# The first sum of weight blocks follows its first low part at once on VectorE, and the third query group is copied one tile sooner

## The chip, the cores and the metric

The kernel runs on one core of a Trainium2 chip. The metric is device time in microseconds; lower is better. The time before is the median of three runs.

Engine names as in the profile: PE is TensorE's matmul side, PEld its weight loads, DVE is VectorE, ACT is ScalarE, POOL is GpSimd, and SP issues DMAs (its queue is SPq).

## What is computed

A trunk of two residual layers over 256 tokens of width 2048, in float32. Layer 0 mixes the tokens by stick-breaking attention (16 heads), layer 1 by a selected sparse softmax attention with 16 query heads in four groups, each group with one key and value head. After each mixer comes an MLP with a squared ReLU. Cut to what matters:

```python
for i in range(DEPTH):                       # DEPTH = 2
    h = rms_norm(x, norm_mix[i])
    x = x + (stick_breaking_mixer(h, w_in_a, w_out_a) if i % 2 == 0 else
             dsa_mixer(h, w_in_b, w_out_b, q_norm_b, k_norm_b, rel_bias))
    h = rms_norm(x, norm_mlp[i])
    x = x + jnp.square(jax.nn.relu(h @ w_up[i])) @ w_down[i]     # 2048 -> 8192 -> 2048
return x
```

## The kernel before

**High and low parts.** Every weight tile (128 x 1024 float32, 512 KB) comes by DMA as a raw tile. ACT copies it to a rounded format as its high part (`wh`, line 121, called by `high`), DVE subtracts that from the raw tile and leaves the low part (`wl`, line 1200, in `low`). PE multiplies by the high part first, then by the low part. Activations are split alike, so a product is three matmuls where a plain one would be one.

**Items.** The whole program is a list of items, each one weight tile with its matmuls. A main loop walks the list. At item i it traces the low part of item i + 3, then loads, then the high part of item i + 4, then the matmuls of item i, and then the steps posted to item i. The traced order is not the order of issue: a planner with a model of the times orders each engine's instructions afterwards, and takes, when an engine comes free in the model, the ready instruction that was traced first. `keep_in_program_order` (here also `pin`) fixes one instruction behind the one traced just before it on the same engine, in issue order alone; it adds no wait. From item 16 on low parts are not fixed. Each engine carries out its own stream in order.

**Groups by halves.** An MLP's hidden width is worked in eight tiles of 1024. The first is done plainly. Each of the seven others (function `seven`, once per f in 1 to 7, in both layers: 14 groups) forms its up-projection from halves of the width and of the tokens, with seven products in place of eight, from sums of weight blocks and sums of activation blocks. Such a group goes over the width in four steps. A step's first half has four items, called here A, B, C and D:

- A uses the block `b11` as loaded (raw tile in `wraw`), into `pair(0)` of an `acc` tile;
- B uses `b22` as loaded (`sraw`), with summed activations `xS`, into the `aux` tile "v";
- C uses b11 + b12, made in place in b11's tile by `two` (line 503), with `xS`, into the `aux` tile "z";
- D uses b12 + b22, made in b12's tile by `other` (line 507), into `pair(1)`. After D's low part comes `three` (line 511), which adds b11 to b22's tile.

Before the change `two` is the source function of item C: it is called when C's high part is made, in `high`. A source function returns the tile that ACT then copies. The last sums, line 514, belong to the second half of a group.

Items of the down-projection (here d) are spread among these: two steps run A B d C D d, and the next two A d B C D and A d B C D d, with one more d between and behind them. In the last step a hidden tile made before is split too: ACT copies its high part (line 605) and DVE subtracts (line 606), each fixed in program order; by the items' due times its first half is traced after the low part of the d that follows A, and before B's low part.

**The second mixer.** Its queries come in four groups of heads, n = 0 to 3. For a group, counted from the last item e of its projection, steps are posted: the tile goes out to DRAM and back (`square`, `away`, `back` at e + 3, 4, 6), `q_turn` copies it to `qTb` on ACT (line 204, fixed behind the `wh` copy that was traced just before), `logits_step` makes the logits (PE line 1033, DVE lines 1035 to 1041, ACT line 1038), `turn_step` transposes the weights (PE line 1050, ACT line 121, DVE line 1053), and `o_step` multiplies by the values (PE lines 1065 to 1067), after which ACT copies the output's high part into `oT` and DVE makes its low part (line 1070). The distances of the last four stand in `STEPS[n]`. The fourth group isn't sent through DRAM; PE transposes it (line 1008). All these steps take their PSUM tiles from `aux`, which has two buffers, given out in traced order. A first item of the output projection (`out_proj`, `acc<-wh,oT`) follows the last query item; items 12 to 17 of it read the third group's heads, those from 18 on the fourth group's.

e is item 39 counted from the first of the key projection for the third group, and 47 for the fourth; so `o_step` of the third group is posted to item 39 + 16 = 55, and `logits_step` of the fourth to 47 + 7 = 54.

Of the kernel before, what the change touches and what calls it, by code (L numbers as in the profile page):

```python
# [8 lines left out]
F32 = mybir.dt.float32  # L9
# [25 lines left out]
BUCKET_FROM = list(range(8)) + [8, 12, 16, 23, 32, 46, 64, 91]  # L35

REL = 383
STEPS = ((11, 12, 16, 18), (11, 12, 15, 17), (10, 11, 14, 16), (3, 7, 11, 15))
BIAS = ((16, 25, 26), (18, 29, 31), (32, 40, 42), (41, 47, 49))
NORMED = (3, 4, 6, 9)  # L40
BORDER = (2, 3, 6, 9)
# [30 lines left out]
class Raw:  # L72


    def __init__(self, src, a, b, tag="wraw"):
        self.src, self.a, self.b, self.tag, self.last, self.ap = src, a, b, tag, None, None


class Item:


    def __init__(self, raws, a, b, mm, moving=False, source=None):
        self.raws, self.a, self.b, self.mm, self.moving, self.post = raws, a, b, mm, moving, []
        self.source, self.then, self.us = source or (lambda: raws[0].ap), None, 2.72
        self.before = None


def plain(src, a, b, mm, moving=False):
# [4 lines left out]
def trunk(ctx, tc, x, xf, gain_cols, w_in_a, w_out_a, w_in_b, w_out_b, rel_bias, w_up, w_down, out):  # L93
# [18 lines left out]
    act, dve, pool, pe = nc.scalar, nc.vector, nc.gpsimd, nc.tensor  # L112

    pinned = [True]

    def pin(ins):
        if pinned[0]:
            tc.keep_in_program_order(ins)
# [260 lines left out]
    def mlp(l, next_col):  # L379
# [79 lines left out]
        def seven(f, c0):  # L459
# [3 lines left out]
            summed = lambda n: lambda kt, part: sec["xS"][:, n, kt, part, :]  # L463

            def block(k, n, s, tag):
                return Raw(rows(w, 1024 * (s // 2) + 512 * k + 256 * (s % 2), 256, c0 + 512 * n, 512), KB, 512, tag)

            def item(raws, bank, x, s, source, opens=True):
                def mm(wh, wl):
                    acc = bank()  # L470
                    on = dict(skip_group_check=not opens)
                    for w, parts in ((wh, (0, 1)), (wl, (0,))):
                        for j in range(KB):
                            k = KB * s + j
                            for part in parts:
                                pe.matmul(acc, x(k, part), w[:, j, :],  # L476
                                          start=opens and w is wh and part == 0 and k == 0,
                                          stop=w is wl and k == HK - 1, **on)
                it = Item(raws, KB, 512, mm, True, source)
                it.us /= 2  # L480
                return it

            def pair(n):
                def bank():
                    if "pair" not in g:
                        g["pair"] = accp.tile([P, 2, 512], F32, name="acc")
                    return g["pair"][:, n, :]
                return bank

            def single(name):  # L490
                def bank():
                    if name not in g:
                        g[name] = auxp.tile([P, 512], F32, name="aux")
                    return g[name]
                return bank

            first, second = [], []
            for s in range(HK // KB):
                b11, b12 = block(0, 0, s, "wraw"), block(0, 1, s, "sraw")
                b21, b22 = block(1, 0, s, "sraw"), block(1, 1, s, "sraw")  # L500

                def two(b11=b11, b12=b12):
                    dve.tensor_add(b11.ap, b11.ap, b12.ap)  # L503
                    return b11.ap

                def other(b12=b12, b22=b22):
                    dve.tensor_add(b12.ap, b12.ap, b22.ap)
                    return b12.ap

                def three(b11=b11, b22=b22):  # L510
                    dve.tensor_add(b22.ap, b11.ap, b22.ap)

                def last_sum(b21=b21, b22=b22):
                    dve.tensor_add(b21.ap, b22.ap, b21.ap)  # L514
                    return b21.ap

                first += [item([b11], pair(0), quarter(0, 0), s, lambda b=b11: b.ap),
                          item([b22], single("v"), summed(3), s, lambda b=b22: b.ap),
                          item([b12], single("z"), summed(0), s, two),
                          item([], pair(1), summed(2), s, other)]  # L520
                first[-1].then, first[-1].uses = three, [b11, b12, b22]
                second += [item([b21], single("y"), quarter(1, 0), s, lambda b=b21: b.ap, False),
                           item([], pair(0), summed(1), s, lambda b=b22: b.ap, False),
                           item([], pair(1), quarter(1, 1), s, last_sum, False)]
                second[-1].uses = [b21, b22]
# [159 lines left out]
        items, late = ds[:16 - EARLY], []  # L685
        ds = ds[16 - EARLY:]
        for f in range(1, LASTF + 1):
            first, second, mid, ends = seven(f, 1024 * f)
            n1, n2, n3 = SPAN.get(f, (9, 2, 5))
            items += spread(first, ds[:n1])  # L690
            put(items, len(items) - 1, mid[:1])
            items += ds[n1:n1 + n2]
            put(items, len(items) - n2, mid[1:])
            items += spread(second, ds[n1 + n2:n1 + n2 + n3])
            late.append((len(items) - 1, ends))
            ds = ds[n1 + n2 + n3:]
# [165 lines left out]
    def mixer_b():  # L862
# [228 lines left out]
        def at(i, f, *a):  # L1091
            items[i].post.append(lambda: f(*a))

        def path(e, key, plan, ready, *a):
            for d, f in zip(plan, ("square", "away", "back")):
                at(e + d, lambda f=f: getattr(st[key], f)())
            at(e + plan[3], ready, *a)
# [11 lines left out]
        for n in range(4):  # L1109
            for d, f in zip(BIAS[n], (lambda n=n: bias_load(n), lambda n=n: bias_mask(n, 0), lambda n=n: bias_mask(n, 2))):  # L1110
                at(k0 + d, f)
            if ("qn", n) in SQUARED:
                path(ends[n], ("qn", n), NORMED[:3] + STEPS[n][:1], q_turn, n)
            else:
                at(ends[n] + STEPS[n][0], q_turn, n)
            for d, f in zip(STEPS[n][1:], (logits_step, turn_step, o_step)):
                at(ends[n] + d, f, n)
# [4 lines left out]
    items = [it for sec in sections for it in sec[0]]  # L1122
# [53 lines left out]
    def half(it, name, bufs):  # L1176
        home = wpool.tile([P, WT + BANK], F32R, name=name, bufs=bufs)
        at = SHIFT
        return home[:, at:at + it.a * it.b].rearrange("p (a b) -> p a b", a=it.a)
# [15 lines left out]
    def low(i):  # L1195
        if i < len(items):
            it = items[i]
            wh, raw = parts[i]
            wl = half(it, "wl", LEAD + 1)
            pin(dve.tensor_sub(wl, raw, wh.bitcast(F32)))  # L1200
            parts[i] = wh, wl
            if it.then:
                it.then()
# [14 lines left out]
    for i in range(LEAD):  # L1218
        high(i)
        if i:  # L1220
            low(i)
        loads(i, 1)
        if i == 1:
            fit((3,))
    high(LEAD)
    section, side = None, features
    for i, it in enumerate(items):
        if i in other:
            side.__exit__(None, None, None)
            side = tc.tile_pool(name=f"side{i}", bufs=1, reuse_waits="tile", side="right")  # L1230
            right[:] = [side.__enter__()]
        if i in left:
            if section is not None:
                section.__exit__(None, None, None)
                if opening is not None:
                    opening.__exit__(None, None, None)
                    opening = None
            section = tc.tile_pool(name=f"section{i}", bufs=1, reuse_waits="tile")
            now[:] = [section.__enter__()]
            left[i](now[0])  # L1240
        pinned[0] = i < PINNED
        low(i + LEAD)
        loads(i + LEAD)
        high(i + LEAD + 1)
        for f in seeds.get(i, ()):
            f()
        it.mm(*parts.pop(i))
        for f in todo.pop(i, []) + it.post:
            f()
# [32 lines left out]
```

## Time and profile before

| | us |
|---|---|
| time, median of 3 runs | 2030.28 (2030.26 to 2030.61) |
| the profiled execution | 2030.05 |
| its span (first to last instruction) | 2028.3 |
| granted TensorE clock | 1.0 |

The profile is of one execution. Busy times are sums over an engine's instructions; matmuls overlap, since each is listed with its latency (0.39 us), while their starts lie 0.227 us apart, so a stretch of PE is read by starts. A row of the timeline holds the start, the duration, the engine (SPq and the like for a queue), the line, the operation, the tiles written and read, the shapes and the count of merged instructions; in brackets stands the idle time of the engine before it, with what ended it. A row of the view of waits holds the waiting engine, tile and line, the releaser, and then the total, the count and the longest, in us and times.

In the groups by halves DVE is the next busiest engine: between 538 and 620 us, one group's period, PE is busy 81.67 of 82.00 us, DVE 76.65 and ACT 60.24.

### The profile page before, as it was taken

To read this page: it belongs to the slowest core of one execution; us is meant where nothing else is said; L and a number is where in the kernel's file an instruction comes from. 1 tells how busy PE (TensorE), PEld (TensorE's weight loads), DVE (VectorE), ACT (ScalarE), POOL (GpSimd) and SP (SyncE) were. 2 spreads that over 40 slices of the span, in tenths; PEclk is the share of its full clock that TensorE was granted. 3 is DMA by queue.
4 is the path that set the end of the run, shared out by engine and by line. 5 is a ranking of instruction groups with operands and counts; after the bars stand their busy time and mean duration, and the time that the engine had idled before them with its cause. 6 is when DMAs were issued, how large, how long until landed. Compare 5 with 4: busy or idle time off the path is not lost.

```text
span 2028.3 us, 25979 instructions
## 1 busy us (share of the span) xinstructions
PE 2018.1 (99%) x9160; PEld 1668.6 (82%) x9160; DVE 1646.0 (81%) x1751; ACT 1361.8 (67%) x1819; POOL 27.7 (1%) x71
## 2 busy tenths in 40 slices
PE   9999999999999999999999999999999999999999
PEld 8888888888888888888888788888888888888887
DVE  5555655898998999989765787689899998999974
ACT  6545555677776776777774656576778677777774
POOL 0101000000000000000000000000000000000000
PEclk9999999999999999999999999999999999999999
DMA  9688865866766858767477876475585876857844
GB/s 323 196 255 224 234 197 168 263 230 207 261 196 225 274 183 260 221 212 251 161 226 207 230 236 199 140 224 196 202 287 173 263 235 210 267 190 229 264 159 137
DMA packets 282116, 447.10 MB, mean 220 GB/s; under 512 B 19008, under 2 KB 88960, under 8 KB 281984
## 3 DMA queue, kind: packets, MB, share of 16 engines
q1 hardware_dynamic: 273840, 437.71, 67.5%
q10 hardware_dynamic: 8144, 7.71, 1.4%
q8 instruction: 72, 1.18, 0.2%
q14 instruction: 60, 0.49, 0.1%
HBM read 416.99 MB, written 28.30 MB: 220 GB/s over the span
## 4 chain that ended last, share of the span: by engine, by line
PE 93%; DVE 2%; DMA 2%; issue 1%; ACT 1%; SPq 0%; DVEq 0%; ACTq 0%
PE acc L320 62%; PE acc L476 13%; PE aux L476 10%; PE acc L343 4%; DVE wraw L503 1%; ACT wh L121 1%; DVE wl L1200 1%; DMA sraw<-hd 1%; DMA hd<-se 1%; PE aux L320 1%; PE aux L1033 0%; DMA wraw<-in_w_down_dram 0%; PE acc L740 0%; PE aux L786 0%; PE acc L938 0%
## 5 line engine op out<-in xcount | busy, mean ns | idle before, releaser
L1200 DVE TENSOR_TENSOR wl<-wraw,wh 128x1024 fp32r<-128x1024 f32 x625 | 755.6, 1219 | 211.4 <-PE acc L320 171.3
L121 ACT ACTIVATE wh<-wraw 128x1024 fp32r<-128x1024 f32 (+1 forms) x627 | 653.5, 1056 | 306.0 <-PE acc L320 207.8
L320 PE MATMUL acc<-wh,hS 128*128 128x512 f32 x2016 | 507.1, 389 | 0.0
L320 PEld LDWEIGHTS acc<-wh,hS 128*128 128x128 f32 x2016 | 378.2, 188 | 78.7
L1200 DVE TENSOR_TENSOR wl<-sraw,wh 128x1024 fp32r<-128x1024 f32 x280 | 339.1, 1221 | 66.7 <-ACT wh L121 34.6
L121 ACT ACTIVATE wh<-sraw 128x1024 fp32r<-128x1024 f32 x280 | 289.9, 1055 | 94.8 <-DVE sraw L514 62.6
L320 PE MATMUL acc<-wh,xT 128*128 128x512 f32 x1280 | 325.7, 392 | 0.2 <-ACT wh L121 0.2
L320 PEld LDWEIGHTS acc<-wh,xT 128*128 128x128 f32 x1280 | 238.0, 188 | 51.4 <-issue 2.3
L320 PE MATMUL acc<-wl,hS 128*128 128x512 f32 x1008 | 267.9, 389 | 0.0
L320 PEld LDWEIGHTS acc<-wl,hS 128*128 128x128 f32 x1008 | 189.1, 188 | 39.2
L320 PE MATMUL acc<-wl,xT 128*128 128x512 f32 x640 | 173.4, 391 | 0.0
L320 PEld LDWEIGHTS acc<-wl,xT 128*128 128x128 f32 x640 | 119.9, 188 | 25.0 <-issue 0.3
L320 PE MATMUL acc<-wh,oT 128*128 128x512 f32 x512 | 132.3, 394 | 0.7 <-ACT oT L121 0.7
L476 PE MATMUL aux<-wh,xS 128*128 128x512 f32 x448 | 121.5, 393 | 3.8 <-ACT wh L121 3.8
L476 PE MATMUL acc<-wh,xS 128*128 128x512 f32 x448 | 120.7, 390 | 0.2
L476 PE MATMUL acc<-wh,xT 128*128 128x512 f32 x448 | 120.4, 389 | 0.0
L121 ACT ACTIVATE xs<-acc 128x512 f32<-128x512 f32 x112 | 60.8, 597 | 85.3 <-PE acc L320 85.2
L320 PEld LDWEIGHTS acc<-wh,oT 128*128 128x128 f32 x512 | 95.0, 188 | 20.2 <-ACT oT L121 1.2
L476 PEld LDWEIGHTS aux<-wh,xS 128*128 128x128 f32 x448 | 82.9, 188 | 25.6 <-ACT wh L121 8.9
L476 PEld LDWEIGHTS acc<-wh,xS 128*128 128x128 f32 x448 | 83.9, 188 | 18.5 <-ACT wh L121 1.1
L476 PEld LDWEIGHTS acc<-wh,xT 128*128 128x128 f32 x448 | 83.9, 188 | 17.4
L343 PE MATMUL acc<-xT,wh 128*128 128x512 f32 x256 | 90.5, 396 | 0.0
(216 smaller groups left out, 2119.8 us busy)
## 6 DMA issues: line engine op xcount, KB each, us to landing
wraw<-in_w_down_dram SPq DMA_DIRECT2D x256, 512.0 KB, 5.0
sraw<-in_w_up_dram SPq DMA_DIRECT2D x168, 512.0 KB, 5.1
wraw<-in_w_in_a_dram SPq DMA_DIRECT2D x95, 512.0 KB, 5.4
wraw<-in_w_up_dram SPq DMA_DIRECT2D x88, 512.0 KB, 4.2
wraw<-in_w_in_b_dram SPq DMA_DIRECT2D x64, 512.0 KB, 4.3
wraw<-in_w_out_a_dram SPq DMA_DIRECT2D x32, 512.0 KB, 4.3
wraw<-in_w_out_b_dram SPq DMA_DIRECT2D x32, 512.0 KB, 3.8
sraw<-hd SPq DMA_DIRECT2D x120, 128.0 KB, 5.5
```

The lines of the kernel that those rows point to most:

```text
L121: pin(act.activation(o, i, AF.Copy, scale=scale))
L320: pin(pe.matmul(acc[t], lhs(k, part, slice(t * P, (t + 1) * P)), w[:, j, :], start=not seed and w is wh and part == 0 and k == 0, stop=w i ...
L343: pe.matmul(acc[:, m, cs], w[:, j, m * P:(m + 1) * P], xT[:, k, xs_, :], start=w is wh and k == 0, stop=w is wl and k == KT - 1)
L476: pe.matmul(acc, x(k, part), w[:, j, :], start=opens and w is wh and part == 0 and k == 0, stop=w is wl and k == HK - 1, **on)
L503: dve.tensor_add(b11.ap, b11.ap, b12.ap)
L1200: pin(dve.tensor_sub(wl, raw, wh.bitcast(F32)))
```

## The change

Two edits. First, `two` is no longer the source of item C. It becomes what is done after A's low part: `low` calls it right after tracing that subtraction, and it is fixed there. The next item's low part is fixed behind it (`sums` marks A for this). C's source now only names b11's tile. Second, `STEPS[2]` is one less in each place: the third group's `q_turn`, `logits_step`, `turn_step` and `o_step` are posted to one item earlier, 48, 49, 52 and 54. At item 54 its `o_step` stands ahead of the fourth group's `logits_step`, since posts of one item are kept in the order in which they were added, by n.

```diff
-STEPS = ((11, 12, 16, 18), (11, 12, 15, 17), (10, 11, 14, 16), (3, 7, 11, 15))
+STEPS = ((11, 12, 16, 18), (11, 12, 15, 17), (9, 10, 13, 15), (3, 7, 11, 15))
...
-        self.before = None
+        self.before, self.sums = None, False
...
                 def two(b11=b11, b12=b12):
-                    dve.tensor_add(b11.ap, b11.ap, b12.ap)
-                    return b11.ap
+                    tc.keep_in_program_order(dve.tensor_add(b11.ap, b11.ap, b12.ap))
...
-                          item([b12], single("z"), summed(0), s, two),
+                          item([b12], single("z"), summed(0), s, lambda b=b11: b.ap),
                           item([], pair(1), summed(2), s, other)]
+                first[-4].then, first[-4].sums = two, True
                 first[-1].then, first[-1].uses = three, [b11, b12, b22]
...
-            pin(dve.tensor_sub(wl, raw, wh.bitcast(F32)))
+            lo = dve.tensor_sub(wl, raw, wh.bitcast(F32))
+            if pinned[0] or items[i - 1].sums:
+                tc.keep_in_program_order(lo)
             parts[i] = wh, wl
             if it.then:
                 it.then()
```

## The prediction

> **What bounds the kernel now.** I read the page's busy times first, then what TensorE waits for, then the timeline around such a wait, one engine at a time.
>
> ```profile
> span 2028.3 us, 25979 instructions
> PE 2018.1 (99%) x9160; PEld 1668.6 (82%) x9160; DVE 1646.0 (81%) x1751; ACT 1361.8 (67%) x1819; POOL 27.7 (1%) x71
> ```
>
> TensorE (PE) is the bound: idle for 2028.3 − 2018.1 = 10.2 us of the span. Neither part of the change takes a matmul away, so what it can give is a piece of those 10.2 us, and whatever slower pace comes with each wait. The view of PE's waits says who causes them:
>
> ```profile
> PE aux L476 <- ACT wh L121: 3.8, 12, 0.3
> PE aux L1216 <- POOL onesf L141: 1.2, 1, 1.2
> PE acc L320 <- ACT oT L121: 0.7, 1, 0.7
> ```
>
> The first row holds twelve waits of a third of a microsecond, in the groups by halves (L476 is their matmul); the third is one wait of the second output projection (`oT`). The edits touch exactly these two; the rest of the 10.2 us stays.
>
> One of the twelve, in the last step of a group (A, B, C, D are a step's four items, d a down item). VectorE (DVE) in that stretch:
>
> ```profile
> 608.60 2.36 DVE L1200 TENSOR_TENSOR wl<-wraw,wh 128x1024 fp32r<-128x1024 f32 x2
> 610.87 1.22 DVE L1200 TENSOR_TENSOR wl<-sraw,wh 128x1024 fp32r<-128x1024 f32 x1
> 612.01 1.22 DVE L503 TENSOR_TENSOR wraw<-wraw,sraw 128x1024 f32<-128x1024 f32 x1
> 613.14 1.22 DVE L606 TENSOR_TENSOR hS<-sraw,hS 128x1024 fp32r<-128x1024 f32 x1
> ```
>
> These are, in order: the low parts of A and of the down item behind it (x2), the low part of B (source `sraw`), the sum `two` (L503), then a low part of the hidden tile (L606). Starts lie 1.14 us apart, and DVE has no gap. ScalarE (ACT) beside it, and then PE:
>
> ```profile
> 610.75 1.09 ACT L121 ACTIVATE xs<-acc 128x512 f32<-128x512 f32 x2 [1.98 <-PE acc L320]
> 611.72 1.06 ACT L605 ACTIVATE hS<-sraw 128x1024 fp32r<-128x1024 f32 x1
> 613.32 1.06 ACT L121 ACTIVATE wh<-wraw 128x1024 fp32r<-128x1024 f32 x1 [0.54 <-DVE wraw L503]
> ```
>
> ```profile
> 611.91 1.07 PE L476 MATMUL aux<-wh,xS 128*128 128x512 f32 x4
> 612.82 0.61 PE L476 MATMUL acc<-wl,xT 128*128 128x512 f32 x2
> 613.27 0.39 PE L320 MATMUL acc<-wh,hS 128*128 128x512 f32 x1
> 613.50 0.61 PE L476 MATMUL aux<-wl,xS 128*128 128x512 f32 x2
> 614.44 1.19 PE L476 MATMUL aux<-wh,xS 128*128 128x512 f32 x4 [0.33 <-ACT wh L121]
> 615.47 0.85 PE L320 MATMUL acc<-wh,hS 128*128 128x512 f32 x3
> ```
>
> The chain is DVE's sum (ends 613.23), ACT's high part of C (613.32 to 614.38), PE at 614.44. The reader should see that nothing in it is slow; the sum merely stands third behind two low parts that PE wants later (that of the down item) or at 613.5 (that of B).
>
> **What one such wait costs.** Four matmuls take 612.82 − 611.91 = 0.91 us unhindered, 0.227 each. From 613.50, two would let C start at 613.95; it starts at 614.44, 0.49 late. C's four then take 615.47 − 614.44 = 1.03, 0.12 more than 0.91. So the wait costs 0.61, 0.28 beyond the 0.33 that the profile calls idle. For all twelve: 3.8 + 12 × 0.28 = 7.2 us.
>
> **Part one, the sum behind A's low part.** The work on DVE is the same: 56 sums, none added. In the stretch above the order becomes low A, sum, low d, low B. With the starts of the rows the sum begins at 609.74 (608.60 + 2.36 − 1.22) instead of 612.01 and ends at 610.96. ACT can then copy C's high part behind the copies that it does anyway: even last in line, behind the hidden tile's, it runs from 612.78 (611.72 + 1.06) to 613.84, and with the 0.06 us between the end of a copy (614.38) and PE's start (614.44) C is free at 613.90, before the 613.95 at which PE gets there. Worth: −7.2 us.
>
> What is late next is B's low part. It moves one place back, from 610.87 to 612.01, ends at 613.23, and reaches PE at 613.29:
>
> ```profile
> 613.27 0.41 PEld L476 LDWEIGHTS aux<-wl,xS 128*128 128x128 f32 x2
> ```
>
> PE's first load for it is at 613.27, so it is missed by 0.02 us. A delay of that size can hide, or can break the overlap of load and matmul (0.12 above). I take 0.05 a group, 12 × 0.05 = +0.6; the ends are 0 and 12 × (0.02 + 0.12) = 1.7. In steps two and three there is room. In step three B's low part ends at 601.73; a place of 1.14 later it ends at 602.87, against 605.11. In step two it ends at 590.91, 2.4 us ahead of its matmul, where a place of 1.14 fits too (step one has the order of step two and is taken alike):
>
> ```profile
> 600.51 1.22 DVE L1200 TENSOR_TENSOR wl<-sraw,wh 128x1024 fp32r<-128x1024 f32 x1
> ```
>
> ```profile
> 605.11 0.62 PE L476 MATMUL aux<-wl,xS 128*128 128x512 f32 x2
> ```
>
> ```profile
> 589.70 1.21 DVE L1200 TENSOR_TENSOR wl<-sraw,wh 128x1024 fp32r<-128x1024 f32 x1
> ```
>
> ```profile
> 593.32 0.62 PE L476 MATMUL aux<-wl,xS 128*128 128x512 f32 x2
> ```
>
> The sum, now fixed in DVE's order, needs the raw block of C. If that were late, every low part behind it would wait, and PE with them. The view of tile `sraw`, for 538 to 590 us:
>
> ```profile
> L1156 SPq DMA_DIRECT2D sraw<-in_w_up_dram x8: 368/368/467, 539.0 to 584.6; - x8
> ```
>
> ```profile
> DMA to landing us min/median/max: 3.4/4.6/7.0
> ```
>
> These eight are the group's blocks for B and C. The last is issued at 584.6 and lands by 591.6, 18 us ahead of the new place of the last sum; so the wait costs nothing. No DMA is issued sooner, and SP's queue is not passed.
>
> A rule of the Trainium skill speaks against this term: "VectorE: DVE Perf Modes", section "The DRAIN you can't avoid", says that the next operation doesn't start until the pipe is empty, so four operations of 1.22 would end B's low part at 608.60 + 4.88 = 613.48. Here starts are 1.14 apart; by that rule it would come 0.25 later, as in the second rival.
>
> **Part two, the third query group a tile sooner.** Its output step is the one wait on `oT`:
>
> ```profile
> 1295.28 0.40 PE L1067 MATMUL aux<-ph,vl 128*128 128x512 f32 x1
> 1296.39 0.49 PE L320 MATMUL acc<-wh,oT 128*128 128x512 f32 x1 [0.71 <-ACT oT L121]
> ```
>
> ```profile
> 1295.76 0.57 ACT L121 ACTIVATE oT<-aux 128x512 fp32r<-128x512 f32 x1
> ```
>
> ```profile
> 1287.73 0.69 DVE L1053 TENSOR_TENSOR pl<-aux,ph 128x512 fp32r<-128x512 f32 x1
> ```
>
> PE ends this step's matmuls and wants the result at once; ACT's copy lies between. A next matmul was due at 1295.28 + 0.23 = 1295.51, so 0.88 is lost, with the slow restart (0.12) 1.0. The step's inputs were ready at 1288.4, yet in the order of the program it stood behind the fourth group's logits, which share the two `aux` buffers. A tile sooner both are posted behind the same item and the third group's step comes first (its posts are appended first). It then has the three logits sums behind it as cover before item 12 needs `oT`: −1.0 us. If that cover fails, the wait stays as it is, +0.
>
> The copy itself goes before one `wh` copy on ACT, that of 1256.45:
>
> ```profile
> 1253.68 1.06 ACT L121 ACTIVATE wh<-wraw 128x1024 fp32r<-128x1024 f32 x1 [1.66 <-PE acc L320]
> ...
> 1256.45 1.06 ACT L121 ACTIVATE wh<-wraw 128x1024 fp32r<-128x1024 f32 x1
> 1257.42 1.14 ACT L204 ACTIVATE qTb<-traw,gains 128x1024 f32<-128x1024 f32 x1
> ```
>
> ```profile
> 1251.51 1.80 SPq L200 DMA_DIRECT2D traw<-hd  x4
> ```
>
> ```profile
> DMA to landing us min/median/max: 2.3/2.5/2.6
> ```
>
> The last of its four loads is issued at 1251.51 + 1.80 × 3/4 = 1252.9 and lands by 1252.9 + 2.6 = 1255.5, so ACT waits 0.8 us from 1254.74 and the copy ends at 1256.6. Queued behind it are the `wh` copy, 0.15 late, and the fourth group's squares; that `wh` is four items ahead of PE, some 10 us, so this costs nothing. The step of the fourth group may slip by the nine matmuls that now pass its logits, 9 × 0.227 = 2.0 us; there is room for 3.0 between its last low part (1314.67) and the item that reads it:
>
> ```profile
> 1313.98 0.69 DVE L1070 TENSOR_TENSOR oT<-aux,oT 128x512 fp32r<-128x512 f32 x1 [1.67 <-ACT oT L121]
> ```
>
> ```profile
> 1317.69 1.07 PE L320 MATMUL acc<-wh,oT 128*128 128x512 f32 x4
> ```
>
> **The sum.** The profiled execution took 2030.05 us (its span and 1.75 around it), 0.2 below the median of 2030.28. 2030.05 − 7.2 + 0.6 − 1.0 = 2022.45, against the median some 2022.5: 0.4% less.
>
> **The rivals.**
> *The sum moves and C's copy doesn't.* ACT's copy of C still follows the hidden tile's copies; behind both, not the first alone, it starts no sooner than now. For it: the planner puts copies in the order of its own model. Against it: the row at 613.32 waited for the sum, not for ACT. Then only part two is left: 2029.
>
> *B's low part is late by more than it looks.* Every group loses 0.25 + 0.02 there: 12 × 0.27 = 3.2 instead of 0.6, 2025.1. The starts 1.14 apart speak against it. (The rule above would give this.)
>
> *Slower: L606 gets in ahead of B's low part.* In the traced order L606 precedes it, and its place is open once the down item's low part ends at 612.1. It needs the hidden tile's copy, which ends at 612.78; if DVE's order has it there, DVE waits until then, B's low part runs 613.9 to 615.2, and PE stands from 613.27 to 615.2, 1.95 + 0.28 = 2.2 instead of 0.61. Twelve groups: +19, less 1.0: 2048. It decides when L606 takes the 612.01 place. Against it: at 612.01 the planner now takes the sum although L606 was traced sooner, so to it L606 isn't ready.
>
> **How the numbers follow.** Forecast 0.62 (2020.9 to 2024.5). B late 0.11; C's copy not moved, or the gain given back by a new order elsewhere, 0.18 (2027 to 2031); slower 0.09. The low end has no delay of B (2021.85) and loses two more waits, at the first group of each layer, which hang on another sum; by the ratio 0.61 to 0.75 of one wait of the twelve (8.9 / 12 on the weight loads) they are worth 1.1 × 0.81 = 0.9:
>
> ```profile
> PEld aux L476 <- ACT wh L121: 8.9, 12, 0.8
> ...
> PEld acc L476 <- ACT wh L121: 1.1, 2, 0.5
> ```
>
> The range 2020.9 to 2030.0 leaves out the slower case and half of the third. A measurement here can tell 0.2%, 4.1 us: faster is below 2026.2, so 0.73, same 0.18, slower 0.09.
>
> **What would show it.** Right: no PE wait at L476 for `wh` of 0.3 (the row of twelve gone), L503 directly behind the first `wl<-wraw` in each step, the ACT row with L503 as releaser gone, no PE wait on `oT`, the wait of PE's weight loads at `aux` under 0.1 each. Wrong: PE waits at `wl` (L1200) instead, L606 ahead of B's low part, or the same twelve waits with the sum moved.

## The result, and the profile after

| | before | after |
|---|---|---|
| time, median of 6 runs each, us | 2030.27 (2029.47 to 2031.23) | 2046.38 (2045.72 to 2052.18) |
| ratio, 95% interval | | 1.0084 [1.0071, 1.0097] |
| the profiled execution, us | 2030.05 | 2046.7 |
| its span, us | 2028.3 | 2045.0 |
| granted TensorE clock | 1.0 | 1.0 |

Times here and below are medians; one execution of an experiment below took 5272 us and is left out of its figures.

The changed kernel is 16.1 us slower, where 7.8 us faster was forecast. The page of the changed kernel, busy times:

```profile
span 2045.0 us, 25885 instructions
PE 2021.7 (99%) x9160; PEld 1666.9 (82%) x9160; DVE 1647.2 (81%) x1751; ACT 1366.8 (67%) x1819; POOL 27.4 (1%) x71
```

Idle time of PE rose from 10.2 to 2045.0 − 2021.7 = 23.3 us. PE's busy time rose too, by 3.6, which is the slower pace next to each wait. The view of PE's waits says where (total, count, longest):

```profile
PE acc L476 <- ACT wh L121: 15.2, 14, 1.3
PE acc L320 <- ACT wh L121: 1.3, 1, 1.3
PE aux L1218 <- POOL onesf L141: 1.2, 1, 1.2
```

The old row of twelve (`aux`, 3.8) and the wait on `oT` are gone. In their place, at the matmuls of a group that write `acc`, stands a wait of up to 1.3 us. It is at item D, once in each of twelve groups, the second to the seventh of each layer. (The second row is one wait that begins 7.9 us after the start, at the first weights; its size differs from trace to trace, 0.2 in that of before.) The last step of one group in the changed kernel, VectorE:

```profile
611.79 1.21 DVE L1200 TENSOR_TENSOR wl<-wraw,wh 128x1024 fp32r<-128x1024 f32 x1
613.04 1.23 DVE L503 TENSOR_TENSOR wraw<-wraw,sraw 128x1024 f32<-128x1024 f32 x1
614.18 1.22 DVE L1200 TENSOR_TENSOR wl<-wraw,wh 128x1024 fp32r<-128x1024 f32 x1
615.32 1.22 DVE L1200 TENSOR_TENSOR wl<-sraw,wh 128x1024 fp32r<-128x1024 f32 x1
616.45 1.22 DVE L506 TENSOR_TENSOR sraw<-sraw 128x1024 f32<-128x1024 f32 x1
617.59 1.22 DVE L606 TENSOR_TENSOR hS<-sraw,hS 128x1024 fp32r<-128x1024 f32 x1
```

The sum (L503) stands directly behind A's low part, ahead of those of d and B. But behind B's low part comes D's sum (`other`, now L506), and only then the hidden tile's low part (L606). Before, L606 came first (613.14, shown in the prediction) and D's sum behind it:

```profile
614.28 1.22 DVE L507 TENSOR_TENSOR sraw<-sraw 128x1024 f32<-128x1024 f32 x1
```

ScalarE and TensorE beside it, after:

```profile
613.44 1.09 ACT L121 ACTIVATE xs<-acc 128x512 f32<-128x512 f32 x2 [2.11 <-PE acc L320]
614.41 1.07 ACT L605 ACTIVATE hS<-sraw 128x1024 fp32r<-128x1024 f32 x1
615.37 1.06 ACT L121 ACTIVATE wh<-wraw 128x1024 fp32r<-128x1024 f32 x1
616.32 1.06 ACT L605 ACTIVATE hS<-sraw 128x1024 fp32r<-128x1024 f32 x1
617.26 1.06 ACT L121 ACTIVATE wh<-wraw 128x1024 fp32r<-128x1024 f32 x1
618.21 1.05 ACT L121 ACTIVATE wh<-sraw 128x1024 fp32r<-128x1024 f32 x1
```

```profile
615.51 0.62 PE L476 MATMUL acc<-wl,xT 128*128 128x512 f32 x2
615.96 0.39 PE L320 MATMUL acc<-wh,hS 128*128 128x512 f32 x1
616.48 1.20 PE L476 MATMUL aux<-wh,xS 128*128 128x512 f32 x4
617.52 0.62 PE L476 MATMUL aux<-wl,xS 128*128 128x512 f32 x2
619.32 1.20 PE L476 MATMUL acc<-wh,xS 128*128 128x512 f32 x4 [1.18 <-ACT wh L121]
620.35 1.75 PE L320 MATMUL acc<-wh,hS 128*128 128x512 f32 x7
```

PE's order has changed too. Before it ran A's low part, one matmul of d, B's low part, C, then the other seven of d with its low part, the eight high ones of the next down item, C's low part, and only then D (L476, into `acc`):

```profile
620.25 1.07 PE L476 MATMUL acc<-wh,xS 128*128 128x512 f32 x4
```

Now C stands ahead of B's low part, and D ahead of d's seven. D's high part is the seventh copy (the sixth row) in a run on ACT that can only begin when PE ends an earlier `acc` tile (the row at 613.44 waits for it); it is copied from 618.21 to 619.26, and PE, which would have come at 617.97, stands until 619.32. D's sum had ended at 617.67, so the copy waited for its turn on ACT and not for the sum.

The loss of one group by starts: at D 619.32 − 617.52 − 0.45 = 1.35, and 0.12 in the four matmuls that follow (620.35 − 619.32 = 1.03 instead of 0.91), 1.47; at C 616.48 − 615.96 − 0.23 = 0.29, and again 0.12, 0.41. Together 1.88 against 0.61 before, +1.27. Counted from C to the next group's C it is a little more:

```profile
696.68 1.21 PE L476 MATMUL aux<-wh,xS 128*128 128x512 f32 x4 [0.33 <-ACT wh L121]
```

```profile
700.06 1.20 PE L476 MATMUL aux<-wh,xS 128*128 128x512 f32 x4
```

Before 696.68 − 614.44 = 82.24, after (second fence) 700.06 − 616.48 = 83.58: +1.34 a group, twelve times 16.1. The rest of the program nearly cancels: by the starts of matmuls with the same number from the beginning, +0.8 in the first 50 us, +0.5 in the first group of layer 0 and nothing in that of layer 1, −1.0 in the second mixer.

### The profile page after: what moved, and what is told of

It reads as the page before. It is cut to its first block, busy times and chain, and to the rows that moved or that the text cites. A ratio compares the mean times of both kernels' runs of the same rounds, so it can differ in the third digit from the quotient of the medians.

```text
span 2045.0 us, 25885 instructions
## 1 busy us (share of the span) xinstructions
PE 2021.7 (99%) x9160; PEld 1666.9 (82%) x9160; DVE 1647.2 (81%) x1751; ACT 1366.8 (67%) x1819; POOL 27.4 (1%) x71
## 4 chain that ended last, share of the span: by engine, by line
PE 85%; DMA 5%; ACT 4%; DVE 3%; issue 2%; SPq 0%; ACTq 0%; DVEq 0%
PE acc L320 58%; PE acc L476 12%; PE aux L476 7%; PE acc L343 4%; DMA wraw<-in_w_down_dram 2%; DVE wl L1200 2%; ACT wh L121 2%; DMA sraw<-hd 1%; DMA hd<-se 1%; ACT sraw L565 1%; DVE wraw L503 1%; PE aux L320 1%; PE aux L1033 1%; DVE sraw L506 0%; ACT hS L605 0%
## 5 line engine op out<-in xcount | busy, mean ns | idle before, releaser
L476 PE MATMUL acc<-wh,xS 128*128 128x512 f32 x448 | 123.0, 395 | 15.2 <-ACT wh L121 15.2
L476 PE MATMUL aux<-wh,xS 128*128 128x512 f32 x448 | 123.0, 393 | 1.5
L476 PE MATMUL acc<-wh,xT 128*128 128x512 f32 x448 | 120.4, 389 | 0.0
L476 PEld LDWEIGHTS acc<-wh,xS 128*128 128x128 f32 x448 | 81.9, 188 | 39.0 <-ACT wh L121 23.2
L476 PEld LDWEIGHTS aux<-wh,xS 128*128 128x128 f32 x448 | 83.2, 188 | 23.5 <-ACT wh L121 6.6
L476 PEld LDWEIGHTS acc<-wh,xT 128*128 128x128 f32 x448 | 84.0, 188 | 17.4
```

Source lines behind the costliest of these rows:

```text
L476: pe.matmul(acc, x(k, part), w[:, j, :], start=opens and w is wh and part == 0 and k == 0, stop=w is wl and k == HK - 1, **on)
```

## The experiments

Each was timed against runs of the kernel before on the same chip, in three sets. That kernel's median was 2030.46 in the first (part two alone, the last step alone, and the two of "D's sum or PE's order"), 2030.29 in the second (part one alone, steps one to three, and the first two of "The price of the twelve waits") and 2029.98 in the third (the repeat, step one, step three).

**Which part, which step.** Part two alone:

```diff
-STEPS = ((11, 12, 16, 18), (11, 12, 15, 17), (10, 11, 14, 16), (3, 7, 11, 15))
+STEPS = ((11, 12, 16, 18), (11, 12, 15, 17), (9, 10, 13, 15), (3, 7, 11, 15))
```

> Part two alone (the sum as before). Both theories on the groups expect the twelve waits of before unchanged (3.8 us of PE idle at aux, 7.2 us lost), and the third query group's wait on oT gone, so 1.0 us less than before: about 2029.3. If part two took a share of the loss, this run would be above 2030.3.

Measured 2028.87 (2028.43 to 2029.71), ratio 0.9993 [0.9983, 1.0002]. Its waits of PE:

```profile
PE aux L476 <- ACT wh L121: 3.8, 12, 0.3
```

The twelve are as before, and no wait on `oT` is listed. −1.6 by medians, against −1.0 forecast; the interval holds zero too.

Part one alone (the changed kernel with the old `STEPS`):

```diff
-STEPS = ((11, 12, 16, 18), (11, 12, 15, 17), (9, 10, 13, 15), (3, 7, 11, 15))
+STEPS = ((11, 12, 16, 18), (11, 12, 15, 17), (10, 11, 14, 16), (3, 7, 11, 15))
```

> The sum moved in all steps, the third query group as before. Theory one (part two is worth -1.0 to -1.6 by itself and doesn't meet part one): 2046.4 + 1.0 = 2047.4, 2046.5 to 2048.5, with the wait of PE on oT of 0.7 back. Rival (the two parts collide in the second mixer): at or below the time of the whole change, 2046 or less.

Measured 2047.9 (2046.93 to 2048.06), ratio 1.0085 [1.0072, 1.0098], with the wait on `oT` back:

```profile
PE acc L320 <- ACT oT L121: 0.7, 1, 0.7
```

So the parts add, and the whole loss belongs to the sum. By the starts, the second mixer is 1.0 shorter with part two alone, 1.0 shorter in the changed kernel, and as long as before with part one alone. Next the sum moved in the last step of a group alone (part two kept, here and below):

```diff
+                soon = s == 3
...
-                          item([b12], single("z"), summed(0), s, lambda b=b11: b.ap),
+                          item([b12], single("z"), summed(0), s, (lambda b=b11: b.ap) if soon else two),
...
-                first[-4].then, first[-4].sums = two, True
+                if soon:
+                    first[-4].then, first[-4].sums = two, True
```

> The sum is moved in the last step of each group alone, part two as in the change. If the loss sits where the hidden tile's low part (L606) shares DVE with the step, the time stays that of the change, about 2046. If the first three steps carry part of it (24 or more lost places on DVE), it falls toward 2030 by their share.

Measured 2045.26 (2044.35 to 2047.06), ratio 1.0074 [1.0059, 1.0089]. Moved there alone, the sum makes nearly all of the loss; that the other steps are free doesn't follow, as is seen below.

**D's sum or PE's order.** The whole change, with D's sum in the last step fixed behind the hidden tile's first low part on VectorE, and nothing said of PE:

```diff
+                    ins = dve.tensor_add(b12.ap, b12.ap, b22.ap)
+                    if s == 3 and split:
+                        tc.add_manual_dep(ins.ins, split[0], mybir.DependencyInfo(
+                            mybir.DependencyClass.NoSync, mybir.DependencyReason.DATA), reason="behind")
```

> The change, with D's sum (b12 + b22) of the last step fixed behind the hidden tile's first low part on DVE. Theory one, that D's sum took the place of that low part and the d item's other seven matmuls wait for it: no PE wait at D, the small one at C (0.4 a group) left, 12 x 1.46 = 17.5 us less than the change less its profiled start-up: about 2027. Theory two, that the planner's PE order alone (D ahead of d) makes the loss: PE's order has D behind d here too, so it expects 2027 as well, and the next run tells them apart. Theory three, that the low part of B comes late: a PE wait at wl stays, above 2040.

Measured 2028.03 (2027.38 to 2029.3), ratio 0.9988 [0.9979, 0.9998]. One pair of VectorE's instructions is in its old order again, and 18 us are gone. On PE (its timeline) d's seven matmuls stand ahead of D again:

```profile
614.52 0.39 PE L320 MATMUL acc<-wh,hS 128*128 128x512 f32 x1
615.04 1.20 PE L476 MATMUL aux<-wh,xS 128*128 128x512 f32 x4
616.07 0.62 PE L476 MATMUL aux<-wl,xS 128*128 128x512 f32 x2
616.53 1.75 PE L320 MATMUL acc<-wh,hS 128*128 128x512 f32 x7
```

The other way round: VectorE's order as in the change, and D's first matmul in the last step fixed behind what was traced before it on PE, so that d's seven come first:

```diff
+                                if behind and w is wh and j == part == 0:
+                                    tc.keep_in_program_order(ins)
...
-                          item([], pair(1), summed(2), s, other)]
+                          item([], pair(1), summed(2), s, other, behind=s == 3)]
```

> The change, with D's first matmul of the last step fixed behind the matmuls traced before it on PE; DVE's order stays that of the change (D's sum ahead of L606). Theory one: PE stands at d instead of D, for L606, from 617.97 to 618.87 in the change's times, 1.0 with the restart in place of 1.46, so about 5.5 us less than the change: 2041. Theory two (order on PE alone): all of 17.5 us is gone, about 2028.

Measured 2038.8 (2038.15 to 2040.96), ratio 1.0043 [1.0028, 1.0058]. Its row of twelve is a new one:

```profile
PE acc L320 <- DVE hS L608: 7.6, 12, 0.7
```

(L608 is that kernel's L606.) The time is 2.2 below theory one's 2041; in two of the twelve groups the wait is 0.2 and not 0.7, which makes up half of that. With d's seven ahead of D again, they wait for the late low part, 10.8 us more than with that low part in its old place (2038.8 − 2028.0). The planner's own order avoids that wait by taking D first, and pays 7.6 more (2046.4 − 2038.8), in D's wait for ACT.

**The price of the twelve waits.** What is left in the kernel with D's sum behind the hidden low part is C's 0.29 + 0.12, since C stands ahead of B's low part on PE. So its edit was kept, and VectorE's order in the last step fixed as low A, sum, low B, low d, hidden low, D's sum. `low` holds the low part of d back until that of B is traced, and puts each behind the one before it (`after` fixes an order on the engine, as `add_manual_dep` above):

```diff
+            if items[i - 1].sums is True and not held:
+                held.append(i)
+                return
...
+            if held and held[0] == i - 1:
+                after(lo, summed_by[0])
+                summed_by.append(lo.ins.name)
+                low(held[0])
+                held.clear()
+            elif held and held[0] == i:
+                after(lo, summed_by[1])
```

> The change with three things fixed in the last step of a group: DVE's order is low A, sum, low B, low d, hidden low part, D's sum (so the low part of B overtakes that of d, which only the seven later matmuls of d need). Theory one (the loss came from D's sum in the hidden low part's DVE place, and what is left with D's sum behind it, 0.4 a group at C, comes from B's low part one place later, for which C was planned ahead of B's low matmuls): B's low part has its old place, C comes behind B's low matmuls with its copy done, so the twelve waits for the high part of C go: 2028.0 - 12 x 0.4 = 2023.2, 2022 to 2025. Rival (C's copy on ACT stays behind the hidden tile's copies, whatever DVE does): the waits stay, 2027 to 2029. Rival two (the low part of d, now third, is late for d's matmuls): new waits of PE at d, over 2030.

Measured 2025.91 (2025.38 to 2027.59), ratio 0.9979 [0.997, 0.9987]. C's wait is gone, as theory one said, but the time is 0.9 above its range and 2.7 above its number. In ten groups d's weight loads now wait for the hidden low part:

```profile
PEld acc L320 <- DVE hS L611: 4.2, 10, 0.5
```

```profile
613.59 1.07 PE L476 MATMUL aux<-wh,xS 128*128 128x512 f32 x4
614.66 1.89 PE L320 MATMUL acc<-wh,hS 128*128 128x512 f32 x7
```

By starts d comes 614.66 − 613.59 − 0.91 = 0.16 late there, and its seven take 0.12 more than the 1.77 of the fastest kernel below: 0.28 a group, 2.8 in ten.

The same with the sum moved in the last step alone (`soon = s == 3`, as above):

> As the kernel with low A, sum, low B, low d in the last step, but the sum moved in that step alone; steps one to three of a group have the order of before. If steps one to three are neutral, as theory one says (there is room of 2 us there), the same time as that kernel within 1 us. If moving the sum there costs something too, this one is faster by it, by 2 us or more.

Measured 2021.51 (2021.09 to 2022.91, five executions; 2021.71 with the one left out), ratio 0.9956 [0.9943, 0.9969]. Once more:

> The same kernel as the fastest so far (low A, sum, low B, low d, hidden low part, D's sum in the last step alone), once more: 2021.7 within 0.7 us, the twelve waits at C gone, each group of the twelve 0.61 shorter than with part two alone.

Measured 2021.82 (2021.57 to 2022.29), ratio 0.996 [0.9948, 0.9973]: faster than both kernels of this study, and the row of twelve waits is not there. VectorE and PE there:

```profile
608.74 1.21 DVE L1222 TENSOR_TENSOR wl<-wraw,wh 128x1024 fp32r<-128x1024 f32 x1
609.99 1.23 DVE L505 TENSOR_TENSOR wraw<-wraw,sraw 128x1024 f32<-128x1024 f32 x1
611.13 1.22 DVE L1222 TENSOR_TENSOR wl<-sraw,wh 128x1024 fp32r<-128x1024 f32 x1
612.27 1.22 DVE L1222 TENSOR_TENSOR wl<-wraw,wh 128x1024 fp32r<-128x1024 f32 x1
613.40 1.22 DVE L616 TENSOR_TENSOR hS<-sraw,hS 128x1024 fp32r<-128x1024 f32 x1
614.54 1.21 DVE L512 TENSOR_TENSOR sraw<-sraw 128x1024 f32<-128x1024 f32 x1
```

```profile
613.40 0.39 PE L320 MATMUL acc<-wh,hS 128*128 128x512 f32 x1
613.63 0.62 PE L476 MATMUL aux<-wl,xS 128*128 128x512 f32 x2
614.09 1.09 PE L476 MATMUL aux<-wh,xS 128*128 128x512 f32 x4
615.01 1.77 PE L320 MATMUL acc<-wh,hS 128*128 128x512 f32 x7
```

(L505 is the sum, L616 the hidden low part, L512 D's sum.) PE has no gap ahead of C, and C's four take 0.92. From group to group each of the twelve is 0.56 to 0.64 shorter than with part two alone: the 0.61 of the prediction.

**What the other steps cost.** This kernel and the one before it, with the sum moved in all steps, differ by 4.1 to 4.4 us, though only steps one to three differ. The sum moved in those three alone:

```diff
-                soon = s == 3
+                soon = s < 3
```

> The sum moved in steps one to three of a group, and left as C's source in the last step; the third query group a tile sooner is kept. Theory one (only the last step loses): the time of part two alone, 2028.9, within 1 us, the twelve waits at the high part of C of 0.3 as before. Rival (the earlier steps carry part of the 16 us): 2031 or more.

Measured 2034.95 (2033.76 to 2036.61), ratio 1.0023 [1.0014, 1.0032]: 6.1 above part two alone. The rival held. In that kernel the last step is planned as before, and yet its waits have grown:

```profile
PE aux L476 <- ACT wh L121: 9.2, 12, 0.8
```

Before the change the sum stood behind B's low part in step one (574.54, 575.68), but ahead of it in step two (588.60; B's low part at 589.70 is shown in the prediction). L583 is a transpose:

```profile
574.54 1.23 DVE L1200 TENSOR_TENSOR wl<-sraw,wh 128x1024 fp32r<-128x1024 f32 x1
575.68 1.22 DVE L503 TENSOR_TENSOR wraw<-wraw,sraw 128x1024 f32<-128x1024 f32 x1
...
588.60 1.18 DVE L503 TENSOR_TENSOR wraw<-wraw,sraw 128x1024 f32<-128x1024 f32 x1
590.83 0.70 DVE L583 STREAM_TRANSPOSE jc<-sraw 128x512 f32<-128x512 f32 x1
```

So step two wasn't run alone, and steps one and three were parted, first one (`soon = s == 0`):

> The sum moved in step one of a group alone, the other three as before; the third query group a tile sooner is kept. Theory (with the sum moved there VectorE gets to a transpose of the squares sooner than ScalarE has made the last square, idles 0.8, and so brings the last step's sum 0.6 later against TensorE; the twelve waits at C grow from 0.49 + 0.12 to 1.1): all the loss of the kernel with steps one to three, 2034 to 2036, the 0.8 idle on VectorE there. Rival (step three, where the sum waits for the low part just ahead of it, carries it): 2029.

Measured 2036.0 (2035.34 to 2036.7), ratio 1.003 [1.0019, 1.0042]: all the loss of the three, at the edge of what was expected. The waits at C:

```profile
PE aux L476 <- ACT wh L121: 9.0, 12, 0.9
```

VectorE in step two of this kernel, and ScalarE beside it:

```profile
586.86 1.18 DVE L1206 TENSOR_TENSOR wl<-wraw,wh 128x1024 fp32r<-128x1024 f32 x1
587.96 0.70 DVE L589 STREAM_TRANSPOSE se<-sraw 128x512 f32<-128x512 f32 x1
589.47 0.71 DVE L589 STREAM_TRANSPOSE jc<-sraw 128x512 f32<-128x512 f32 x1 [0.81 <-ACT sraw L571]
```

```profile
588.30 1.14 ACT L571 ACTIVATE sraw<-jc 128x512 f32<-128x512 f32 x1
```

L589 turns the squares of the tile made before (L583 in the changed kernel), L571 makes them. VectorE now reaches the last transpose before the square is made, and idles 0.81. Before, the sum and a low part of step two stood ahead of that transpose (588.60 to 590.83 above), and no such wait was listed. In the changed kernel it is there as well, in its view of VectorE's waits:

```profile
DVE jc L583 <- ACT sraw L565: 8.1, 10, 0.8
```

VectorE runs without another long gap from there to the last step, so all of that step's sums and low parts come later against PE. The twelve groups bear this out: ten have the idle, and C's wait there is 0.83 to 0.85; the second group of each layer doesn't, and its wait is 0.27, as with part two alone. Every kernel here with the sum moved in step one has the idle in these ten groups (they are also the ten of d's wait for the hidden low part above), and no other kernel has it. Step three alone (`soon = s == 2`):

> The sum moved in step three of a group alone. Theory (step one carries the loss; in step three the sum starts 1.25 instead of 1.14 behind the low part, and what follows loses as much less): 2028.9 within 1 us, as with part two alone. Rival (step three carries it): 2034 to 2036.

Measured 2031.29 (2029.82 to 2032.3), ratio 1.0005 [0.9996, 1.0014]: neither theory's number, though it parts them.

```profile
PE aux L476 <- ACT wh L121: 5.9, 12, 0.5
```

The longest wait at C went from 0.33 to 0.49, some 0.16 × 12 = 1.9 us. That I had put at nothing, and where the 0.16 comes from wasn't followed. Step one is the larger: by starts over the twelve groups it costs 7.3 against part two alone, step three 2.0, and the three steps together 6.4. They don't add: with all three moved, C waits 0.82 in the ten groups, no longer than with step one alone.

## Why the prediction was wrong

**What was right.** The sums and their prices: one wait at C costs 0.61, twelve of them 7.3, and they can be had by moving the sum, if its neighbours' order is fixed too (2021.8, against the forecast 2022.5 for the change). ACT's copy of C also came where it was put: forecast to end 613.84 − 610.75 = 3.09 after the `xs` copies begin, measured 616.43 − 613.44 = 2.99. Part two took its wait away: −1.0 forecast, −1.0 by starts in the second mixer; the medians say −1.6 and −1.5 (alone, and beside part one), which by time alone could not be told from zero.

**The step that failed** is "what is late next is B's low part", and with it "C is free at 613.90, before the 613.95 at which PE gets there". The prediction moved one instruction, the sum, and left every other in its order on VectorE and PE. Two things were not followed:

- *D's sum waits for nothing but `two`* (its blocks being loaded; it overwrites b12, which `two` reads). In the prediction's own row of VectorE, L606 stands directly behind L503. When the sum goes two places forward, D's sum becomes ready two places earlier and takes the place before L606. That this place decides is shown by the kernel which only puts D's sum behind L606 again: −18 us. The prediction saw the danger to L606's place in its third rival, but from the wrong side: L606 ahead of B's low part. It used as evidence that "to it L606 isn't ready"; the same sentence, read on, says that another ready instruction would get the place.
- *PE's order was taken as given.* It is planned as well. C went ahead of B's low part, so that PE came to it 0.45 sooner than the forecast's 613.95 and missed the copy by 0.29; D went ahead of d's seven. C's term was −0.61 a group and came out −0.61 + 0.41 = −0.20; D, which the prediction had put at nothing, added +1.47.

Why the planner, in its own model of the times, ranked them so isn't in any trace; that D's sum and L606 were the pair is shown, the model's reason isn't.

**The term for B's low part**, +0.6, never came up: with PE's new order its matmuls come after C, at 617.52, where its low part had ended at 616.54. In the fastest kernel B's low part stands ahead of d's, so no run tests the term.

**"In steps two and three there is room; step one has the order of step two and is taken alike"** failed too, for another reason. The rows of VectorE for step two were misread: B's low part at 589.70 stands behind the sum there already, while in step one it stands ahead of it. The room was measured for B's low part on PE. What moved in step one was VectorE's work between ACT's squares: 0.81 idle there, and with the last step planned as before 6 us. In the change itself the three steps cost less, 2046.4 − 2045.3 = 1.1. That fits with D's wait being set by ACT's run of copies, which begins at PE's release, but no run tests it.

**The rivals.** The slower one came near in size (2048 for 2046.4) by luck, with the wrong mechanism: B's low part wasn't late, and PE never waited on `wl` in the changed kernel. "The sum moves and C's copy doesn't" (2029) was wrong: C's copy moved. The chance of 0.18 named "a new order elsewhere", which is what happened, but priced it at the gain given back and no more (2027 to 2031). The sign by which it was to be judged, L503 behind the first `wl<-wraw` in the last step, was there: a change can do exactly what it says and still lose.

**The sum with what was measured**: 2030.3 + 12 × (0.41 + 1.47 − 0.61) − 1.0 (second mixer) + 0.5 (first group of layer 0) + 0.8 (start) = 2045.8, of 2046.4. The period from C to C grew by 0.07 more than these two waits (1.34 against 1.27, 0.8 over twelve); what makes that up wasn't followed.

## What to carry to other kernels

When an instruction is moved forward, list what waits on it alone: those become ready earlier as well, and in a kernel whose order is planned they take places from work that a busier engine needs first. Follow each engine's order through the stretch, the bound one's too, before a wait is booked as gone; and where one good place is wanted, fix its neighbours as well: here the move in the one step that had the wait, with its neighbours' order fixed (B's low part ahead of d's, D's sum behind the hidden low part), is 8 us faster (2021.8), and with them left free it is 15 us slower (2045.3); part two, some 1 us, is in both. A step in which nothing waits gains nothing from the same edit and may lose by it.

## What the runs showed of the hardware

Two VectorE operations of 128 x 1024 start 1.14 us apart when the second doesn't need the first, and their rows overlap by 0.08. The sum directly behind A's low part, whose operand `wraw` it overwrites, starts later: 609.99 − 608.74 = 1.25 in the fastest kernel, 613.04 − 611.79 = 1.25 in the changed one. Such a pair was 0.11 further apart in each trace that has it. The Trainium skill, "VectorE: DVE Perf Modes", section "The DRAIN you can't avoid", says that a next operation waits for the pipe to empty, that one which isn't held starts earlier, and that a semaphore between two operations costs nothing extra. The first agrees with the dependent pair (0.03 between end and start) and not with the independent ones, which overlap by 0.08 and for which the second speaks; so the section as a whole doesn't give the 0.25 of the prediction's second rival. The third differs from these runs, which show 0.11, if it is the wait on the neighbour that makes them; no run tried the same pair without it.

A wait of PE costs more than its idle time: C's 0.13 of idle in the changed kernel was 0.41 by starts, D's 1.18 was 1.47, and the 0.33 before was 0.61, 0.28 or 0.29 beyond the idle in each. The fastest kernel gave back all 0.61 a group, so the price by starts is the one to book.
